# Attention's value products, low halves, key and query copies rebuilt in a two-layer decoder trunk on one core

## The chip, the cores and the metric

The kernel runs on one core of a Trainium2 chip. The metric is the device time of one execution in microseconds. A core has five engines with a queue of instructions each: TensorE (PE, matmuls; its loads of stationary operands are listed as PEld), VectorE (DVE), ScalarE (ACT), GpSimd (POOL) and SyncE (SP), which here only issues DMAs.

## The reference

512 tokens of width 1024 go through two layers. Layer 0 mixes tokens with a gated MLP in chunks of 128. After it, one shared set of keys and values is computed. Layer 1 attends to it. Both layers also have a gated convolutional MLP of width 2816 and a gated per-layer embedding; everything is float32. The part that the change touches:

```python
kv = rmsnorm(h, g) @ w_kv                       # 4 key/value heads of 64
q = (xn @ w_q).reshape(B, nb, BLOCK, 4, 4, 64)  # 16 query heads, 4 to a group
scores = einsum('bnikgd,bnjkd->bnkgij', q, kblk) * 64 ** -0.5
scores = scores - slopes * dist                 # window of 128, blocks of 128: previous and own
scores = where(valid, scores, -inf)
m = maximum(max(scores, -1), sink)
e = exp(scores - m)
probs = e / (sum(e, -1) + exp(sink - m))
out = einsum('bnkgij,bnjkd->bnikgd', probs, vblk)
return out.reshape(B, S, 1024) @ w_o
```

## The kernel before

Activations lie with features on the partitions and the 512 tokens along the free dimension, as eight row blocks of 128x512. Every float32 product is made of matmuls in the faster float32r form: each operand is split into a high half (the value rounded) and a low half (what is left), and `mm3` adds three products: high by high, high by low, low by high. So one 128x128 block of weights costs three matmuls of 512 columns.

Weights come as a stream of pieces of 1 MB. `load` issues a piece's DMA on SP into one of three raw buffers (two during attention, when the third holds the values). `pump` splits a piece in units of 128x1024: ACT casts the high half `wh` (L141), DVE subtracts for the low half `wl` (L142). There are four buffers for the units of each half, and a product asks for units four ahead.

Layer 1 starts with the key projection `k` (two tiles of 128 features), then the first group's queries `q`. `Norm.split` prepares the queries' input row blocks, `begin` and `rstd` give the norm's factor. Keys are kept per group in `kh` and `kl`: a group's 64 key features stand twice on the 128 partitions, so that a query tile whose upper half holds the high halves and whose lower half holds the low halves is multiplied with both at once. ACT makes both copies of the high halves (L536), DVE one and GpSimd the other copy of the low ones (L538). `queries` scales a query tile (L516) and writes the two halves with ACT (L521) and DVE (L522).

Attention proper has 16 steps, one for each of 4 groups of heads and 4 blocks of tokens, in a software pipeline written out by hand:

- `scores(i)`: two matmuls for each of four heads (L617, L618), then on DVE one instruction per head that adds the distance, scales, and takes the maximum (L620); `neg` (L624); four exponentials on ACT (L627) with their sums.
- `weights(i)`: sums and reciprocal on DVE (L637, L638), then the scaling of four heads, two on DVE (L644) and two on ACT (L642).
- `turn(i-1)`: transposes on PE (L654), then the split of the transposed probabilities into `ph` (ACT, L214) and `pl` (DVE, L215).
- `mix(i-2)`: for each key block three matmuls with 64 value columns (L671 to L673), into 64 partitions; then per head a cast on ACT (L678) and a subtraction on DVE (L679) into the input of the output projection `o2`.

Between these, `fill(i)` takes products that need no result of the step from the table `beside`: the value products (`values`, 256 columns per matmul), the next groups' query products (`project`) and, in the last steps, parts of the output projection (`merge`, tile `o`). After step 16 the rest of the output projection follows, 120 matmuls in a row.

Each engine works through its queue in order. The order in a queue is made ahead of time by the framework: by program order, with parts marked `high_priority` ahead, and by its own estimate of when an instruction can start. So the order on PE mixes fills, logits, transposes and value products.

Of the kernel before, what the change touches and what calls it, by code (L numbers as in the profile page):

```python
# [8 lines left out]
F32 = mybir.dt.float32  # L9
F32R = mybir.dt.float32r  # L10
# [36 lines left out]
def tile_yoco(ctx: ExitStack, tc: tile.TileContext, t, out: bass.AP, out_b: bass.AP):  # L47
# [14 lines left out]
    # ---- weights: a stream of pieces, each loaded once and split in two float32r halves  # L62
    pieces = []

    def plan(ap_, n, cols, own=None):
# [7 lines left out]
        pieces.append((ap_, n, cuts, own))  # L73

    def plan_cols(w, n_chunks, kk, cols=256, k0=0):
        for c in range(n_chunks):
            plan(w[c, :, k0 * cols : (k0 + kk) * cols], kk * cols, cols)
# [26 lines left out]
    plan_cols(t["w_q"][1:4], 3, KD)  # L104
    plan_cols(t["w_o"], 4, KD)
# [22 lines left out]
    def pump(upto):  # L128
        while state["unit"] < min(upto, len(units)):
# [12 lines left out]
            nc.vector.tensor_sub(wl[:, :n], src, wh[:, :n].bitcast(F32))  # L142
# [9 lines left out]
    def chunk(cols, kk, ahead=WBUFS):  # L152
        """The next units that make up kk row blocks of `cols` columns, a triple for each."""
# [8 lines left out]
    def mm3(ps, parts, xs, c0, n=P, first=True, last=True):  # L162
        """ps += W[:, c0:c0+n]^T x over the row blocks, as three float32r passes."""
# [8 lines left out]
    def mm3t(ps, xs, parts, c0, n, tok, first=True, last=True):  # L172
        """ps += x[tokens]^T W[:, c0:c0+n]: tokens on partitions."""
# [9 lines left out]
    # ---- activations in  # L183
# [24 lines left out]
    # ---- helpers on activations  # L208
# [16 lines left out]
    class Norm:  # L225
        """Takes the residual's row blocks as they come: gains and splits them, sums the squares."""
# [24 lines left out]
        def begin(self):  # L251
            """One over the root mean square, tokens on the partitions."""
# [6 lines left out]
        def rstd(self):  # L259
            """The same along the free dimension, for every partition."""  # L260
# [12 lines left out]
    def spread(r, n, name):  # L273
        """[P, n] with tokens on the partitions -> [P, n * P], the tokens along it, in PSUM."""
# [18 lines left out]
    def dense_add(xs, kk, norm):  # L293
        """h += W^T x for the next kk row blocks of weights, 256 columns a chunk."""
# [10 lines left out]
    def ffn(l, norm, nxt):  # L305
        """Gated MLP, the hidden units in parts; the first of the next part goes before a part's products down."""
# [79 lines left out]
    # ---- layer 0: gMLP mixer  # L386
# [26 lines left out]
    # minus the distance to the key, far away where the window or causality forbids it  # L413
# [7 lines left out]
    # queries over eight times a head's slope: logit = slope * (q k - distance)  # L421
# [10 lines left out]
    # positions attend to earlier ones alone: wsT[s, h, t] for s <= t  # L432
# [55 lines left out]
    # ---- layer 1: shared K/V and sliding-window attention  # L488
# [3 lines left out]
    # keys of a group, their halves twice on the partitions, for the stacked halves of the queries  # L492
# [14 lines left out]
    qps = psum("q0_0")  # L507
    mm3(qps, parts, xq, 0)
    rstd = nm.rstd()

    def queries(ps, g, j):
        """Two heads' queries, scaled for the distances; a head's tile has one half on its own
        partitions and the other half on the other's."""
# [3 lines left out]
        res = []  # L517
        for e in range(2):
            q = tp.tile([P, S], F32R, tag=("hs", "sg", "c0", "c1")[2 * j + e], name=f"q{g}_{j}_{e}")
            me, it = sides[e], sides[1 - e]  # L520
            nc.scalar.copy(q[me, :], qf[me, :])  # L521
            nc.vector.tensor_sub(q[it, :], qf[me, :], q[me, :].bitcast(F32))  # L522
            res.append(q)
# [3 lines left out]
    for j in range(2):  # L527
        if j:
            qps = psum("q0_1")
            mm3(qps, parts, xq, P)  # L530
        kf = tp.tile([P, S], F32, tag="acc", name=f"kf{j}")
        nc.vector.tensor_mul(kf, kps[j], rstd)
        for e in range(2):
            me = sides[e]
            for side in (me, sides[1 - e]):
                nc.scalar.copy(kh[j][side, e, :], kf[me, :])  # L536
            for side, eng in ((me, nc.vector), (sides[1 - e], nc.gpsimd)):
                eng.tensor_sub(kl[j][side, e, :], kf[me, :], kh[j][me, e, :].bitcast(F32))  # L538
        qs[0] += queries(qps, 0, j)
    state["tags"] = [0, 1]  # L540

    vt = wp.tile([P, 2, NC, 256], F32R, tag="r2", bufs=1, name="vt")

    # products beside attention's steps: each step is followed by some that need no result of it
    box = {}

    def values(c):
# [4 lines left out]
        nc.scalar.activation(vt[:, 0, c, :], ps[:, :256], AF.Copy, scale=rt[:, c : c + 1])  # L552
        nc.vector.scalar_tensor_tensor(vt[:, 1, c, :], ps[:, :256], rt[:, c : c + 1], vt[:, 0, c, :].bitcast(F32),
# [12 lines left out]
    def merge(m, k0, k1):  # L566
        """Row block m of the output projection, from the heads that are done."""
# [8 lines left out]
        -1: [(values, 0), (values, 1), (project, 1, 0, 0, 8)],  # L576
# [289 lines left out]
```

## Time and profile before

| | |
|---|---|
| median of 3 runs | 1174.45 us (1174.26 to 1174.66) |
| span of the profiled execution | 1173.3 us |
| PE, DVE, ACT, POOL busy | 1152.2, 761.8, 543.0, 80.7 us |
| mean granted TensorE clock | 0.996 |
| instructions | 14202 |

The profiled execution has no time of its own beside its span; the median of the runs is 1.15 us longer. Busy times of PE count overlapping instructions once; a matmul's recorded duration is longer than the distance to the next one. In a group's row, the mean is that of one instruction; the idle time is that of the engine just ahead of the group's instructions, with what ended it.

### The profile page before, as it was taken

Reading aid. Unit: us, or ns where it says so; the run is one execution under the profiler, and the core shown is the slowest. Engines: PE = TensorE matmul, PEld = TensorE weight load, DVE = VectorE, ACT = ScalarE, POOL = GpSimd, SP = SyncE. Lnnn points to the kernel's source line nnn. Section 1 sums busy time; section 2 is a strip of 40 time slices with the busy share of each in tenths; the row PEclk is TensorE's granted clock in tenths of the full one; section 3 lists DMA queues with packets and bytes.
Section 4 is the critical chain, followed back from the end, with each engine's and each line's share of the span. In section 5 each row is a group of like instructions: output and inputs, shape, how many; then the busy total and the mean of one; then the engine's idle time right before and its main releaser. Section 6 shows DMA issues by size and latency. Waiting matters only on the chain.

```text
span 1173.3 us, 14202 instructions
## 1 busy us (share of the span) xinstructions
PE 1152.2 (98%) x5634; PEld 968.3 (83%) x5634; DVE 761.8 (65%) x1229; ACT 543.0 (46%) x919; POOL 80.7 (7%) x86
## 2 busy tenths in 40 slices
PE   7999999999999999999989999999999999999998
PEld 7988888888888888888778767888888888888897
DVE  6365467763676377447779997577635773675665
ACT  5633444431344244445559986444313442345532
POOL 1000210000000000031220001100000000000221
PEclk9999999999999999999989999999999999999999
DMA  8222323322222333232212113322322333223302
GB/s 324 79 108 72 108 72 108 108 74 106 108 72 90 110 104 115 101 111 72 72 37 73 36 37 108 108 97 84 108 107 73 99 99 108 90 94 105 108 1 73
DMA packets 19011, 110.20 MB, mean 94 GB/s; under 512 B 2176, under 2 KB 3584, under 8 KB 8704
## 3 DMA queue, kind: packets, MB, share of 16 engines
q1 hardware_dynamic: 18112, 108.24, 26.5%
q10 hardware_dynamic: 832, 1.05, 0.3%
q8 instruction: 44, 0.72, 0.2%
q14 instruction: 23, 0.19, 0.1%
HBM read 107.19 MB, written 2.10 MB: 93 GB/s over the span
## 4 chain that ended last, share of the span: by engine, by line
PE 90%; DVE 6%; ACT 2%; issue 1%; DMA 0%; SPq 0%; POOLq 0%; POOL 0%; DVEq 0%; ACTq 0%
PE up L168 14%; PE up L170 14%; PE up L169 14%; PE d L168 8%; PE d L170 8%; PE d L169 8%; PE gate L169 2%; PE gate L168 2%; PE gate L170 2%; PE v L179 1%; PE v L180 1%; PE v L181 1%; PE u L168 1%; PE u L170 1%; PE u L169 1%; PE o L168 1%
## 5 line engine op out<-in xcount | busy, mean ns | idle before, releaser
L141 ACT CAST wh<-wraw 128x1024 fp32r<-128x1024 f32 (+1 forms) x198 | 203.0, 1026 | 272.8 <-PE d L169 132.2
L142 DVE TENSOR_TENSOR wl<-wraw,wh 128x1024 fp32r<-128x1024 f32 (+1 forms) x198 | 238.6, 1205 | 134.9 <-ACT wh L141 134.6
L168 PE MATMUL up<-nf00h,wh 128*128 128x512 f32 x352 | 137.2, 390 | 0.0
L168 PE MATMUL up<-nf10h,wh 128*128 128x512 f32 x352 | 137.2, 390 | 0.0
L170 PE MATMUL up<-nf10h,wl 128*128 128x512 f32 x352 | 137.1, 390 | 0.0
L170 PE MATMUL up<-nf00h,wl 128*128 128x512 f32 x352 | 137.1, 389 | 0.0
L169 PE MATMUL up<-nf00l,wh 128*128 128x512 f32 x352 | 137.1, 389 | 0.0
L169 PE MATMUL d<-al,wh 128*128 128x512 f32 x352 | 137.1, 389 | 0.0
L168 PE MATMUL d<-ah,wh 128*128 128x512 f32 x352 | 137.1, 389 | 0.0
L169 PE MATMUL up<-nf10l,wh 128*128 128x512 f32 x352 | 137.1, 389 | 0.0
L170 PE MATMUL d<-ah,wl 128*128 128x512 f32 x352 | 137.1, 389 | 0.0
L325 ACT ACTIVATE c<-hs,vec 128x512 f32<-128x512 f32 x88 | 71.5, 814 | 71.9 <-DVE hs L321 71.1
L326 DVE SCALAR_TENSOR_TENSOR c<-hs,vec,c 128x511 f32<-128x511 f32 x88 | 65.8, 749 | 34.2 <-ACT c L325 34.2
L301 DVE TENSOR_TENSOR h<-h,d 128x512 f32<-128x512 f32 x56 | 38.4, 687 | 73.7 <-PE d L170 73.7
L214 ACT CAST ah<-a 128x512 fp32r<-128x512 f32 x44 | 27.3, 621 | 109.1 <-DVE a L331 109.0
L170 PEld LDWEIGHTS up<-nf10h,wl 128*128 128x128 f32 x352 | 66.1, 188 | 13.8
L170 PEld LDWEIGHTS up<-nf00h,wl 128*128 128x128 f32 x352 | 66.1, 188 | 13.8
L170 PEld LDWEIGHTS d<-ah,wl 128*128 128x128 f32 x352 | 66.1, 188 | 13.7
L169 PEld LDWEIGHTS d<-al,wh 128*128 128x128 f32 x352 | 66.1, 188 | 13.7
L168 PEld LDWEIGHTS up<-nf00h,wh 128*128 128x128 f32 x352 | 66.1, 188 | 13.7
L169 PEld LDWEIGHTS up<-nf10l,wh 128*128 128x128 f32 x352 | 66.1, 188 | 13.6
L168 PEld LDWEIGHTS d<-ah,wh 128*128 128x128 f32 x352 | 66.1, 188 | 13.6
(281 smaller groups left out, 2195.4 us busy)
## 6 DMA issues: line engine op xcount, KB each, us to landing
wraw<-in_w_up SPq DMA_DIRECT2D x44, 1024.0 KB, 4.8
wraw<-in_w_down SPq DMA_DIRECT2D x16, 896.0 KB, 4.6
wraw<-in_w_down SPq DMA_DIRECT2D x8, 1024.0 KB, 4.9
wraw<-in_w_gate SPq DMA_DIRECT2D x8, 1024.0 KB, 4.8
wraw<-in_w_u SPq DMA_DIRECT2D x4, 1024.0 KB, 6.3
wraw<-in_w_out SPq DMA_DIRECT2D x4, 1024.0 KB, 4.7
wraw<-in_w_q SPq DMA_DIRECT2D x4, 1024.0 KB, 4.7
wraw<-in_w_o SPq DMA_DIRECT2D x4, 1024.0 KB, 4.8
```

The lines of the kernel that those rows point to most:

```text
L141: nc.scalar.copy(wh[:, :n], src)
L142: nc.vector.tensor_sub(wl[:, :n], src, wh[:, :n].bitcast(F32))
L168: nc.tensor.matmul(ps, wh[:, a:b], xh, start=st, stop=False)
L169: nc.tensor.matmul(ps, wh[:, a:b], xl, start=False, stop=False)
L170: nc.tensor.matmul(ps, wl[:, a:b], xh, start=False, stop=en)
L179: nc.tensor.matmul(ps, xh[:, s], wh[:, a:b], start=st, stop=False)
L180: nc.tensor.matmul(ps, xl[:, s], wh[:, a:b], start=False, stop=False)
L181: nc.tensor.matmul(ps, xh[:, s], wl[:, a:b], start=False, stop=en)
L214: nc.scalar.copy(hi, src)
L301: nc.vector.tensor_add(h[m], h[m], ps)
L325: nc.scalar.activation(c, hs, AF.Identity, bias=v("conv_b", l * 2 * NJ + col), scale=cw[2])
L326: nc.vector.scalar_tensor_tensor(c[:, 1:], hs[:, : S - 1], cw[1], c[:, 1:], op0=ALU.mult, op1=ALU.add)
```

## The change

- `mix`: the value tile holds a group's high and low halves side by side (`vt` is `[P, NC, GROUPS, 2, HD]`), so that one matmul with 128 stationary columns gives the products with both halves on 128 partitions. Two matmuls per key block in place of three (the low by low product is now included). Then ACT copies the lower 64 partitions (`lo`), DVE adds the two halves into `of` (two additions over two heads each), ACT casts two 128x128 blocks and GpSimd subtracts for their low halves.
- `pump`: for the last three pieces of `w_q` and the four of `w_o` the low halves are subtracted on GpSimd in place of DVE.
- Keys: ACT and DVE write one copy of the halves, and eight DMAs write the other. The two key tiles' products run over row blocks 0 to 5 first and then 6 and 7; both query products of group 0 come before the keys are taken out of PSUM.
- Queries of groups 1 to 3: one cast and one subtraction over the whole tile, then four DMAs to the two heads' tiles. Group 0 is as before.
- The logits are kept negated: the scale's sign is turned, the minimum with `nsink` gives the negated maximum at once, and the exponential has a scale of -1. The instruction `neg` goes.
- `weights`: all four scalings on DVE.
- `beside`: the first query product of group 1 moves from before step 0 to step 0, the second's two parts are joined at step 1.

```diff
-    plan_cols(t["w_q"][1:4], 3, KD)
-    plan_cols(t["w_o"], 4, KD)
+    plan_cols(t["w_q"][1:4], 3, KD, side=True)
+    plan_cols(t["w_o"], 4, KD, side=True)
...
-            nc.vector.tensor_sub(wl[:, :n], src, wh[:, :n].bitcast(F32))
+            (nc.gpsimd if pieces[i][4] else nc.vector).tensor_sub(wl[:, :n], src, wh[:, :n].bitcast(F32))
...
+    nsink = const.tile([P, HEADS], F32, name="nsink")
+    nc.gpsimd.tensor_scalar_mul(nsink, sink, -1.0)
...
-    kps = []
-    for j in range(2):
-        ps = psum(f"k{j}")
-        mm3(ps, parts, xkv, j * P)
-        kps.append(ps)
-        for k in range(4 * j, 4 * j + 4):
-            nm.split(k, 1)
+    kps = [psum(f"k{j}") for j in range(2)]
+    for k0, k1 in ((0, 6), (6, KD)):
+        for j in range(2):
+            mm3(kps[j], parts[k0:k1], xkv[k0:k1], j * P, first=k0 == 0, last=k1 == KD)
+    for k in range(KD):
+        nm.split(k, 1)
     rt = nm.begin()
     parts = chunk(256, KD)
-    qps = psum("q0_0")
-    mm3(qps, parts, xq, 0)
+    qps = [psum(f"q0_{j}") for j in range(2)]
+    mm3(qps[0], parts, xq, 0)
     rstd = nm.rstd()
+    mm3(qps[1], parts, xq, P)
+    for j in range(2):
+        kf = tp.tile([P, S], F32, tag="acc", name=f"kf{j}")
+        nc.vector.tensor_mul(kf, kps[j], rstd)
+        for e in range(2):
+            nc.scalar.copy(kh[j][sides[e], e, :], kf[sides[e], :])
+            nc.sync.dma_start(kh[j][sides[1 - e], e, :].bitcast(F32), kh[j][sides[e], e, :].bitcast(F32))
+        for e in range(2):
+            nc.vector.tensor_sub(kl[j][sides[e], e, :], kf[sides[e], :], kh[j][sides[e], e, :].bitcast(F32))
+            nc.sync.dma_start(kl[j][sides[1 - e], e, :].bitcast(F32), kl[j][sides[e], e, :].bitcast(F32))
...
+        hi = tp.tile([P, S], F32, tag="acc", name=f"qhi{g}_{j}")
+        nc.scalar.copy(hi.bitcast(F32R), qf)
+        nc.vector.tensor_sub(qf.bitcast(F32R), qf, hi)
+        for e, q in enumerate(res):
             me, it = sides[e], sides[1 - e]
-            nc.scalar.copy(q[me, :], qf[me, :])
-            nc.vector.tensor_sub(q[it, :], qf[me, :], q[me, :].bitcast(F32))
-            res.append(q)
+            nc.sync.dma_start(q[me, :].bitcast(F32), hi[me, :])
+            nc.sync.dma_start(q[it, :].bitcast(F32), qf[me, :])
...
-        kf = tp.tile([P, S], F32, tag="acc", name=f"kf{j}")
-        nc.vector.tensor_mul(kf, kps[j], rstd)
-        for e in range(2):
-            me = sides[e]
-            for side in (me, sides[1 - e]):
-                nc.scalar.copy(kh[j][side, e, :], kf[me, :])
-            for side, eng in ((me, nc.vector), (sides[1 - e], nc.gpsimd)):
-                eng.tensor_sub(kl[j][side, e, :], kf[me, :], kh[j][me, e, :].bitcast(F32))
...
-        -1: [(values, 0), (values, 1), (project, 1, 0, 0, 8)],
-        0: [(project, 1, 1, 0, 4)],
-        1: [(project, 1, 1, 4, 8)],
+        -1: [(values, 0), (values, 1)],
+        0: [(project, 1, 0, 0, 8)],
+        1: [(project, 1, 1, 0, 8)],
...
-            nc.vector.tensor_tensor_reduce(out=pr[:, e, :nk], in0=far[:, k0:], in1=o, scale=slope(hd),
-                                           scalar=sink[:, hd : hd + 1], op0=ALU.add, op1=ALU.max,
-                                           accum_out=mx[:, e : e + 1])
-        neg = at.tile([P, GQ], F32, tag="neg", bufs=2, name=f"neg{i}")
-        nc.vector.tensor_scalar_mul(neg, mx, -1.0)
+            nc.vector.tensor_tensor_reduce(out=pr[:, e, :nk], in0=far[:, k0:], in1=o, scale=-slope(hd),
+                                           scalar=nsink[:, hd : hd + 1], op0=ALU.add, op1=ALU.min,
+                                           accum_out=neg[:, e : e + 1])
...
-            if e in (1, 3):
-                nc.scalar.activation(a, a, AF.Copy, scale=r)
-            else:
-                nc.vector.tensor_scalar_mul(a, a, r)
+            nc.vector.tensor_scalar_mul(a, a, r)
...
-            nc.tensor.matmul(ps[:HD, :], vh, ph, start=b == 0, stop=False)
-            nc.tensor.matmul(ps[:HD, :], vh, pl, start=False, stop=False)
-            nc.tensor.matmul(ps[:HD, :], vl, ph, start=False, stop=end)
+            vv = vt[:, c, g].rearrange("p x d -> p (x d)")
+            nc.tensor.matmul(ps, vv, ph, start=b == 0, stop=False)
+            nc.tensor.matmul(ps, vv, pl, start=False, stop=b == len(pts) - 1)
         cols = slice(n * P, (n + 1) * P)
-        for e in range(GQ):
-            oh, ol = o2[2 * g + e // 2]
-            src = ps[:HD, e * P : (e + 1) * P]
-            nc.scalar.copy(oh[sides[e % 2], cols], src)
-            nc.vector.tensor_sub(ol[sides[e % 2], cols], src, oh[sides[e % 2], cols].bitcast(F32))
+        of = at.tile([P, 2, P], F32, tag="of", bufs=1, name=f"of{i}")
+        lo = at.tile([HD, S], F32, tag="olo", bufs=1, name=f"olo{i}")
+        nc.scalar.copy(lo, ps[sides[1], :])
+        halves = [a.rearrange("p (b e t) -> p b e t", b=2, e=2) for a in (ps[sides[0], :], lo)]
+        for e in range(2):
+            nc.vector.tensor_add(of[sides[e]], halves[0][:, :, e, :], halves[1][:, :, e, :])
+        for b in range(2):
+            oh, ol = o2[2 * g + b]
+            nc.scalar.copy(oh[:, cols], of[:, b, :])
+            nc.gpsimd.tensor_sub(ol[:, cols], of[:, b, :], oh[:, cols].bitcast(F32))
```

The rest of the diff takes comments and docstrings out.

More of the change, by code (lines that the diff above doesn't have):

```diff
@@ L63, in tile_yoco, with plan @@
     pieces = []
-    def plan(ap_, n, cols, own=None):
+    def plan(ap_, n, cols, own=None, side=False):
         if own and len(own) > 1:
@@ L516, in queries @@
         nc.vector.scalar_tensor_tensor(qf, ps, qscale[:, m : m + 1], rstd, op0=ALU.mult, op1=ALU.mult)
-        res = []
-        for e in range(2):
-            q = tp.tile([P, S], F32R, tag=("hs", "sg", "c0", "c1")[2 * j + e], name=f"q{g}_{j}_{e}")
+        res = [tp.tile([P, S], F32R, tag=("hs", "sg", "c0", "c1")[2 * j + e], name=f"q{g}_{j}_{e}")
+               for e in range(2)]
+        if g == 0:
+            for e, q in enumerate(res):
+                me, it = sides[e], sides[1 - e]
+                nc.scalar.copy(q[me, :], qf[me, :])
+                nc.vector.tensor_sub(q[it, :], qf[me, :], q[me, :].bitcast(F32))
+            return res
+        hi = tp.tile([P, S], F32, tag="acc", name=f"qhi{g}_{j}")
+        nc.scalar.copy(hi.bitcast(F32R), qf)
+        nc.vector.tensor_sub(qf.bitcast(F32R), qf, hi)
+        for e, q in enumerate(res):
             me, it = sides[e], sides[1 - e]
-            nc.scalar.copy(q[me, :], qf[me, :])
-            nc.vector.tensor_sub(q[it, :], qf[me, :], q[me, :].bitcast(F32))
-            res.append(q)
+            nc.sync.dma_start(q[me, :].bitcast(F32), hi[me, :])
+            nc.sync.dma_start(q[it, :].bitcast(F32), qf[me, :])
         return res
```

26 lines of the change are left out of this document (11 added, 15 removed).

## The prediction

> **What bounds the kernel now.** I read the page's engine shares and clock row first, then the windows by stage, then who TensorE (PE) waited for.
>
> ```profile
> span 1173.3 us, 14202 instructions
> PE 1152.2 (98%) x5634; PEld 968.3 (83%) x5634; DVE 761.8 (65%) x1229; ACT 543.0 (46%) x919; POOL 80.7 (7%) x86
> PEclk9999999999999999999989999999999999999999
> ```
>
> TensorE is busy everywhere; only one slice of 40 shows a lowered clock, near 600 us, where attention begins. The change touches the stretch from the key projection to the output projection, so I cut it into windows. Columns: window, length, then busy time (and instructions) of PE, PEld, DVE, ACT, POOL, the granted clock, DMA share and GB/s.
>
> ```profile
> 200.00:300.00 100.00, 100.00 (x443) 82.86 (x442) 56.81 (x68) 33.21 (x40) 0.00 (x0) 1.00 0.28 101
> ...
> 565.00:601.60 36.60, 32.28 (x169) 26.96 (x167) 31.18 (x44) 21.83 (x32) 10.45 (x7) 0.99 0.10 31
> 600.80:607.60 6.80, 5.97 (x16) 4.91 (x17) 2.91 (x16) 2.44 (x11) 0.00 (x0) 0.50 0.46 154
> 601.60:626.00 24.40, 24.37 (x135) 21.42 (x136) 15.94 (x56) 15.35 (x45) 0.00 (x0) 0.88 0.20 72
> 626.00:674.00 48.00, 46.93 (x258) 36.77 (x256) 45.77 (x159) 42.57 (x135) 0.00 (x0) 1.00 0.15 51
> 674.00:714.00 40.00, 38.25 (x194) 27.90 (x193) 34.50 (x125) 32.59 (x108) 0.00 (x0) 1.00 0.13 41
> 714.00:741.00 27.00, 27.00 (x120) 22.05 (x119) 19.34 (x26) 14.82 (x25) 8.59 (x6) 1.00 0.38 137
> ```
>
> The dense row at 200 gives the true price of a 512-column matmul: 100 us / 443 = 0.226 us (recorded durations near 0.39 us overlap). From 626 to 714 three engines run level: PE 85.2, DVE 80.3, ACT 75.2 of 88 us. So a step of attention has no single limit; PE ends last by a little. The row at 600.8 is the half clock: 6.8 us at 0.50 lose 3.4 us. From 714 on PE is saturated again, with 27 us of output projection that need little of anyone.
>
> ```profile
> PE sc L617 <- DVE mx L620: 2.5, 2, 2.1
> PE sc L617 <- DVE q L522: 2.0, 2, 1.6
> PE gate L169 <- DVE np10l L211: 1.3, 1, 1.3
> PE k L168 <- ACT n10h L210: 0.7, 1, 0.7
> PE sc L617 <- DVE pl L215: 0.4, 1, 0.4
> PE o L168 <- DVE mx L620: 0.4, 1, 0.4
> PE o L168 <- ACT oh L678: 0.3, 1, 0.3
> PE o L168 <- DVE ds L637: 0.2, 1, 0.2
> PE o L168 <- DVE pl L215: 0.2, 1, 0.2
> ```
>
> Columns: waiter and releaser, total, times, longest. Without the gate's row (another stage) PE idles 6.7 us here. The two longest, 1.6 and 2.1, are the first logits, just ahead of the half clock. Hence the start of attention costs 1.6 + 2.1 + 3.4 = 7.1 us, the key projection 0.7, and all later steps together 2.3 of recorded waits.
>
> **The change part by part.** Prices come from the groups of 545 to 725 us (count | busy us, mean ns):
>
> ```profile
> L142 DVE TENSOR_TENSOR wl<-wraw,wh 128x1024 fp32r<-128x1024 f32 x22 | 28.9, 1314 | 1.4 <-ACT wh L141 1.2
> L215 DVE TENSOR_TENSOR pl<-tr,ph 128x512 fp32r<-128x512 f32 x28 | 19.1, 687 | 2.3 <-ACT ph L214 2.1
> L679 DVE TENSOR_TENSOR ol<-pv,oh 64x128 fp32r<-64x128 f32 x64 | 17.3, 280 | 2.8 <-ACT oh L678 1.6
> L671 PE MATMUL pv<-ph,vt 128*64 128x512 f32 x28 | 11.1, 397 | 0.0
> L522 DVE TENSOR_TENSOR q<-qf,q 64x512 fp32r<-64x512 f32 x16 | 12.0, 748 | 0.4
> L642 ACT ACTIVATE pr<-pr,ds 128x256 f32<-128x256 f32 x24 | 10.8, 502 | 1.7 <-DVE ds L638 1.6
> L644 DVE TENSOR_SCALAR pr<-pr,ds 128x256 f32<-128x256 f32 x24 | 7.3, 348 | 0.0
> L538 DVE TENSOR_TENSOR kl<-kf,kh 64x512 fp32r<-64x512 f32 x4 | 5.5, 1374 | 0.1
> L624 DVE TENSOR_SCALAR neg<-mx 128x4 f32<-128x4 f32 x16 | 2.5, 158 | 0.1
> L644 DVE TENSOR_SCALAR pr<-pr,ds 128x128 f32<-128x128 f32 x8 | 1.9, 280 | 0.1
> ```
>
> *Value products in two passes.* The third matmul of each of 28 key blocks goes. The two that stay are as long (512 columns), with 128 weight columns in place of 64. 28 x 0.226 = 6.3 us leave PE. This shortens the span only as far as PE sets the pace: bounds -6.3 and 0; I take -6.3 and charge the other engines' slowness below.
>
> *Combining the halves.* DVE loses 64 subtractions (-17.3) and gains 32 additions of 64x256 with one operand in PSUM. The nearest rows are 280 ns at 128 columns and 687 at 512, so 0.42 us each, +13.3. ACT trades 64 short casts for 16 of 64x512 and 32 of 128x128, about even. The 32 low halves go to GpSimd.
>
> *Weights all on DVE.* 24 x 0.348 + 8 x 0.280 = +10.6 us; ACT loses the same scalings (24 x 0.50 = 12 and eight short ones).
>
> *Negated logits.* 16 x 0.158 = -2.5 us on DVE, taken out of the chain from maximum to exponential; the sink's negation is one small GpSimd instruction in layer 0, long before anyone reads it: nil.
>
> *Weights' low halves on GpSimd.* Seven pieces of two units: 14 x 1.22 (undisturbed, fence below) = -17.1 us on DVE.
>
> *Queries of groups 1 to 3.* 12 half-height subtractions become 6 full ones at 0.69: -4.1 us on DVE.
>
> DVE's sum is 13.3 + 10.6 - 17.3 - 2.5 - 17.1 - 4.1 = -17.1 us, if GpSimd does not disturb it. What GpSimd takes on:
>
> ```profile
> L739 POOL TENSOR_TENSOR facc<-fsq,fsq 128x256 f32<-128x256 f32 x2 | 1.5, 736 | 12.3 <-ACT fsq L732 10.2 <-PE gate L170 2.1
> L244 POOL TENSOR_TENSOR nf1acc<-nf1sq,nf1sq 128x512 f32<-128x512 f32 x1 | 1.3, 1332 | 126.8 <-DVE nf10l L211 126.8
> ```
>
> 736 ns at 256 columns and 1332 at 512 put 1024 columns near 2.6 us and 128 near 0.44: 14 x 2.6 + 32 x 0.44 = 50 us of GpSimd, most of it between 601.6 and 714, where the windows show none now. And a GpSimd instruction is not free for DVE. From two stretches of the timeline (start, duration):
>
> ```profile
> 543.95 1.22 DVE L142 TENSOR_TENSOR wl<-wraw,wh 128x1024 fp32r<-128x1024 f32 x1
> ```
> ```profile
> 546.91 1.33 POOL L244 TENSOR_TENSOR n1acc<-n1acc,n1sq 128x512 f32<-128x512 f32 x1 [4.15 <-ACT n1sq L239]
> ```
> ```profile
> 547.02 2.32 DVE L142 TENSOR_TENSOR wl<-wraw,wh 128x1024 fp32r<-128x1024 f32 x1
> ```
> ```profile
> 566.95 1.53 POOL L244 TENSOR_TENSOR n1acc<-n1acc,n1sq 128x512 f32<-128x512 f32 x1 [3.84 <-ACT n1sq L239]
> ```
> ```profile
> 567.25 0.68 DVE L378 TENSOR_TENSOR z<-gate,np0rstd 128x512 f32<-128x512 f32 x1
> ```
>
> The subtraction that started under the GpSimd addition took 2.32 instead of 1.22 us: it ended 1.1 us after that addition did, as if it had only then begun. The product at 567.25, one operand in PSUM, was not touched. So what reads two SBUF operands waits out GpSimd. In the new step those are the small sums for the denominator and the query subtraction; the new additions and the logits read PSUM. The Trainium skill ("SBUF — State Buffer", section "SBUF: two separate sides") says that the pair of ports is an exclusive lock held for the whole instruction, against DVE instructions with two SBUF inputs and also against those in a two-port mode; the first half agrees with 2.32 beside 1.22, and for the second, which would take in the weights' scalings, no row here has an overlap.
>
> Price: 16 steps lie in those 112 us, 7 us each, with about 2.4 groups of such instructions (denominator's two sums, and six query subtractions over all). A 2.6 us GpSimd instruction is met with a chance near 0.6, for 1.4 us on average: 14 x 0.6 x 1.4 = 12, and 1 for the short ones. Bounds 0 and 50; I take 13, nearest to half of each 2.6. DVE then gets 17.1 - 13 = 4 us shorter while PE gets 6.3 shorter: DVE becomes the engine that ends a step. I hand back the difference of 2.3, and 1.2 for half as many uneven waits again as today's 2.3: +3.5 (bounds -1.5, if those waits shrink instead, and +14).
>
> *Start of attention.* The six first row blocks of both key tiles now run before the last two, which hides PE's 0.7: -0.7. Keys are doubled by eight DMAs instead of ACT and GpSimd copies. The four DVE subtractions at 1374 ns sat under GpSimd's share and return to 0.69, -2.7 us, but two of the weights' low halves now fall there. One group of DMA rows bounds the new latency:
>
> ```profile
> out<-y SPq DMA_DIRECT2D x4, 256.0 KB, 2.5
> ```
>
> That is to DRAM; 128 KB inside SBUF should land in 1.5 to 2.5 us. I take 2. All eight lie beside the remaining query product and the 48 short value products. Moving the next query product (24 x 0.226 = 5.4 us) behind the first logits removes no work; it takes cover from the wait and gives it to the first step. I leave 1.7 of the 3.7 us of idling: -2.0 (bounds -3.7 and +2). With 1.7 us the clock should hold, since the gate's single wait of 1.3 lowered nothing that the clock row shows: -3.4 (bounds -3.4 and 0). The Trainium skill ("TensorE: Matmul & The Clock Gate", section "What's actually happening") puts the drop behind an idle window of about 3.4 us; here 1.6 and 2.1 us with work between them were enough, so by the trace a stall of half that is the safer reading.
>
> *New waits.* The second unit of the third query piece can only be split after the last value product has freed its buffers, and its low half takes 2.6 instead of 1.2 us: +1.0 (0 to +3). Behind a group's last value product stand ACT copy, two additions, cast and a GpSimd subtraction before the output projection may use it, on a PE that is in order: +1.5 (0 to +4). Query DMAs sit in the SP queue among the weight loads, with two steps (14 us) until they are needed: 0. After 714 the 27 us of saturated PE hide the longer last chain: 0.
>
> Sum: -6.3 + 3.5 - 0.7 - 2.0 - 3.4 + 1.0 + 1.5 = -6.4. 1173.3 - 6.4 = 1166.9 of span; the median shown is 1.15 above the profiled span, so 1168.0.
>
> **The rivals.** *GpSimd's lock sets the pace.* If each of the 14 instructions holds DVE for its full 2.6 us, DVE gets 36 - 17 = 19 us longer; between 626 and 714 it has 8 us free, the start still gives about 5: +6, 1180. It decides from about 30 us of holding, 2.1 us per instruction. For it: the lock above, and scalings of all four heads exposed. Against: most of DVE's work reads PSUM. *Queries come late.* SP's queue waits long in front of weight loads:
>
> ```profile
> SPq L124 <- DVE wl L142: 246.8, 18, 30.5
> ```
>
> If a query's copy stands behind such a load, up to 30 us against 14 of slack, PE would stall for 5 to 15 us at two group changes: 1180 to 1195. Against: the queue has nothing else now, so long waits cost nothing and say little on order. *PE keeps the pace.* No hand-back, half the new waits, no idling at the start: -6.3 - 0.7 - 7.1 + 1 = -13.1, 1161. For it: ACT loses 12 us and more of scalings, DVE 17. *Eaten.* DVE or the chain keeps the step as long as before, and the clock still drops: -0.7 - 2 + 1 = -1.7, 1172.7; the change does not reach the span.
>
> **How the numbers follow.** Forecast 0.46, PE keeps the pace 0.17, eaten 0.14 (a third of it beyond the bound), lock 0.13, late queries 0.10. A measurement can tell 0.2%, 2.3 us. Faster 0.68, same 0.10, slower 0.22. The range goes from 1159, below the best case by its bounds, to 1181, past the lock; the forecast's own is 1163 to 1172.
>
> **What would show it.** Right: 28 fewer matmuls; no half clock near 600; DVE groups with SBUF operands lengthened, GpSimd near 55 us; the wait at the first logits under 2 us. Wrong: a clock of 0.50 again after 590; PE waiting for a query's DMA; DVE over 95% busy with denominators of 1 to 2 us; windows from 626 on as long as now.

## The result and the profile after

The changed kernel took 1177.95 us (median of 6 runs, 1177.25 to 1181.8); the kernel before took 1174.68 us beside it. The ratio is 1.0032, 95% interval 1.0022 to 1.0042: slower by 3.3 us, where 6.4 us faster was forecast.

Two profiles were taken of the changed kernel. The first is of the longest execution, 1181.8 us (span 1180.1), which ran 17.1 us at half clock in three stretches, 8.5 us lost. The second, 1176.41 us with a span of 1174.7, lies nearer to the median and is read below as "after". Its busy times:

```profile
PE 1146.4 (98%) x5606; PEld 966.8 (82%) x5606; DVE 760.5 (65%) x1193; ACT 528.6 (45%) x861; POOL 126.2 (11%) x129
```

TensorE has 28 matmuls fewer and 5.8 us less to do, as planned. DVE has 36 instructions fewer, yet its busy time has hardly moved (761.8 before, 760.5 now). GpSimd went from 80.7 to 126.2 us. The prediction's windows, with the same columns, and a last one for the whole stretch from 626:

```profile
565.00:601.60 36.60, 33.10 (x168) 28.55 (x167) 29.36 (x51) 20.79 (x36) 9.73 (x5) 0.95 0.30 87
601.60:626.00 24.40, 22.14 (x139) 19.54 (x138) 18.64 (x52) 13.40 (x36) 4.97 (x3) 1.00 0.24 52
626.00:674.00 48.00, 42.77 (x235) 34.29 (x234) 44.72 (x137) 34.43 (x102) 17.51 (x17) 1.00 0.32 95
674.00:714.00 40.00, 36.06 (x184) 28.33 (x183) 31.63 (x110) 28.55 (x88) 14.14 (x19) 0.96 0.13 40
626.00:714.00 88.00, 78.83 (x416) 62.62 (x415) 76.36 (x246) 62.98 (x189) 31.65 (x36) 0.98 0.23 70
```

From 626 to 674 PE is busy 42.8 us where it had 46.9: it idles. DVE, at 44.7 of 48, has not come down, although ACT now has 8 us less and GpSimd 17.5 us where it had none. The clock is below 1 twice, 0.95 and 0.96: two stretches of 3.4 us at half speed, one from 598 us and one from 683.6. Together they cost what the one stretch of 6.8 us cost before. Who PE waited for (545 to 750 us; total, times, longest):

```profile
PE sc L632 <- DVE neg L635: 10.1, 8, 2.5
PE o L169 <- ACT oh L692: 2.1, 1, 2.1
PE sc L632 <- DVE q L536: 1.0, 1, 1.0
PE sc L632 <- DMA q<-qf: 0.8, 1, 0.8
PE sc L632 <- DVE pl L216: 0.3, 1, 0.3
PE o L170 <- POOL ol L693: 0.3, 1, 0.3
```

These waits make 14.6 us; before they made 6.7. That closes the account: 6.3 us of matmuls gone, 7.9 us of waits added, the loss to the clock the same: +1.6, where the span grew by 1.4. It is the account of this execution; the median run is 1.5 us longer, and the two runs on either side of it have granted clocks of 0.995 and 0.993 beside 0.996 here, so part of that is clock. Most of the new waits are at the logits. These need a bank of PSUM that DVE frees when it has reduced the logits before (`neg`, line 635), and DVE is late. The groups say why:

```profile
L143 POOL TENSOR_TENSOR wl<-wraw,wh 128x1024 fp32r<-128x1024 f32 x14 | 35.0, 2503 | 50.9 <-ACT wh L142 50.9
L654 DVE TENSOR_SCALAR pr<-pr,ds 128x256 f32<-128x256 f32 x48 | 21.3, 501 | 0.2
L693 POOL TENSOR_TENSOR ol<-of,oh 128x128 fp32r<-128x128 f32 x32 | 14.7, 479 | 48.6 <-ACT oh L692 48.6
L689 DVE TENSOR_TENSOR of<-pv,olo 64x256 f32<-64x256 f32 x32 | 13.2, 413 | 3.2 <-POOL ol L693 2.6 <-ACT olo L686 0.2
L650 DVE TENSOR_TENSOR ds<-ds,sm 128x4 f32<-128x4 f32 x16 | 7.3, 462 | 4.2 <-ACT ds L644 3.9
L536 DVE TENSOR_TENSOR q<-qf,q 64x512 fp32r<-64x512 f32 x4 | 5.5, 1364 | 0.8 <-ACT q L535 0.7
```

A sum of four numbers for each partition (line 650) takes 462 ns. The weights' scaling (line 654) takes 501 ns; it took 348. The query subtraction takes 1364; untouched it takes 686 (in a_wl_dve below). The sum took 157 ns before:

```profile
L637 DVE TENSOR_TENSOR ds<-ds,sm 128x4 f32<-128x4 f32 x16 | 2.4, 157 | 3.8 <-ACT ds L631 3.8
```

Over their counts that is 48 x 0.153 + 16 x 0.305 + 4 x 0.678 = 14.9 us, and 0.5 more for the short scalings: DVE is held for 15.4 us. The addition with one operand in PSUM (line 689) takes 413 ns, as priced. One hold can be followed through three engines of this profile (start, duration). GpSimd:

```profile
590.75 5.45 POOL L143 TENSOR_TENSOR wl<-wraw,wh 128x1024 fp32r<-128x1024 f32 x2 [11.14 <-ACT wh L142]
```
```profile
625.96 2.41 POOL L143 TENSOR_TENSOR wl<-wraw,wh 128x1024 fp32r<-128x1024 f32 x1 [6.85 <-ACT wh L142]
628.33 0.98 POOL L693 TENSOR_TENSOR ol<-of,oh 128x128 fp32r<-128x128 f32 x2
629.27 2.42 POOL L143 TENSOR_TENSOR wl<-wraw,wh 128x1024 fp32r<-128x1024 f32 x1
```

DVE, beside these:

```profile
592.64 4.11 DVE L536 TENSOR_TENSOR q<-qf,q 64x512 fp32r<-64x512 f32 x2 [0.69 <-ACT q L535]
```
```profile
626.51 1.88 DVE L650 TENSOR_TENSOR ds<-ds,sm 128x4 f32<-128x4 f32 x1 [0.36 <-ACT ds L644]
628.42 0.18 DVE L651 RECIPROCAL ds<-ds 128x4 f32<-128x4 f32 x1
628.64 3.47 DVE L654 TENSOR_SCALAR pr<-pr,ds 128x256 f32<-128x256 f32 x4
```

PE, behind these:

```profile
594.04 0.33 PE L632 MATMUL sc<-kh,q 128*128 128x128 f32 x1 [1.03 <-DVE q L536]
```
```profile
597.58 0.33 PE L632 MATMUL sc<-kh,q 128*128 128x128 f32 x1 [2.47 <-DVE neg L635]
```
```profile
633.41 0.33 PE L632 MATMUL sc<-kh,q 128*128 128x128 f32 x1 [2.32 <-DVE neg L635]
```
```profile
682.84 0.50 PE L169 MATMUL o<-oh,wh 128*128 128x512 f32 x1 [2.06 <-ACT oh L692]
```

A GpSimd subtraction ran from 625.96 to 628.37. DVE's four-column sum began at 626.51 and ended at 628.39, as that subtraction did. Then came the reciprocal and the four scalings, which are held in turn by the second subtraction, from 629.27 to 631.69 (3.47 us, where four free ones at 606.34 took 1.14). Behind them in DVE's queue, after two other instructions, stood the reduction of the next logits, and PE stood for 2.32 us. At 592.64 it is the same with the two query subtractions: 4.11 us in place of 1.41 for the two before them, PE waits 1.03 and 2.47, and then the clock falls. The last row is another matter: the output projection waits for the chain behind a group's last value product, and the second stretch at half clock follows it.

### The profile page after: what moved, and what is told of

It reads as the page before. It is cut to its first block, busy times and chain, and to the rows that moved or that the text cites. A ratio compares the mean times of both kernels' runs of the same rounds, so it can differ in the third digit from the quotient of the medians.

```text
span 1180.1 us, 14226 instructions
## 1 busy us (share of the span) xinstructions
PE 1151.1 (98%) x5606; PEld 970.3 (82%) x5606; DVE 760.6 (64%) x1193; ACT 528.7 (45%) x861; POOL 126.3 (11%) x129
## 4 chain that ended last, share of the span: by engine, by line
PE 91%; DVE 5%; ACT 2%; issue 1%; DMA 1%; SPq 0%; POOLq 0%; POOL 0%; DVEq 0%; ACTq 0%
PE up L169 14%; PE up L171 14%; PE up L170 14%; PE d L170 8%; PE d L171 8%; PE d L169 8%; PE gate L170 2%; PE gate L169 2%; PE gate L171 2%; PE v L180 1%; PE v L181 1%; PE v L182 1%; PE u L170 1%; PE u L171 1%; PE u L169 1%; DVE pr L654 1%
## 5 line engine op out<-in xcount | busy, mean ns | idle before, releaser
L143 DVE TENSOR_TENSOR wl<-wraw,wh 128x1024 fp32r<-128x1024 f32 (+2 forms) x184 | 221.8, 1206 | 134.4 <-ACT wh L142 134.2
L170 PEld LDWEIGHTS up<-nf00l,wh 128*128 128x128 f32 x352 | 66.1, 188 | 13.6
```

The source lines that it names most:

```text
L143: (nc.gpsimd if pieces[i][4] else nc.vector).tensor_sub(wl[:, :n], src, wh[:, :n].bitcast(F32))
L170: nc.tensor.matmul(ps, wh[:, a:b], xl, start=False, stop=False)
```

## The experiments

**The theories.** The first is the lock: a GpSimd instruction stops DVE's work on SBUF operands until it ends, and DVE's fixed order passes the stop on to PE. The rivals: that scalings which ACT shared are now all on DVE; that the two-pass products trade a dense stretch of PE for a longer chain of additions; that queries or keys come late by DMA. The kernels come in two lines, from the one after and from the one before, and later from the fastest found. The kernel before was run again beside each group of kernels, with medians from 1174.43 to 1174.97 us, so a comparison across groups carries some 0.5 us.

**Low halves back on DVE (a_wl_dve).** One word of the change undone:

```
- (nc.gpsimd if pieces[i][4] else nc.vector).tensor_sub(wl[:, :n], src, ...)
+ nc.vector.tensor_sub(wl[:, :n], src, ...)
```

> The changed kernel with the weights' low halves back on DVE (14 subtractions of 128x1024), all else changed. Theory L (the lock): GpSimd's 14 long instructions hold DVE in lumps of up to 2.5 us (scalings L654 501 ns on average beside 344 undisturbed, sums L650 461 beside 163, query subtractions L536 1360 beside 686: some 15 us in all), and PE, which waits in order for the logits' PSUM, loses the lumps: without them DVE gets 17 us of work and loses 15 us of holding, but evenly; PE's waits at sc fall from 10 us to 3 or 4, time 1169 to 1172. Theory C (the chain): the new step itself (four scalings on DVE, the longer way through the halves' addition) makes DVE late; then DVE only gets more work and the time stays at 1177 to 1180. Theory Q (queries by DMA): no change, 1177 to 1179.

Measured: 1169.14 us, ratio 0.9950 (0.9937 to 0.9962), 8.8 us below the changed kernel and within the lock's forecast. Its busy times and groups:

```profile
PE 1145.0 (98%) x5606; PEld 965.8 (83%) x5606; DVE 760.7 (65%) x1207; ACT 530.1 (45%) x861; POOL 92.7 (8%) x115
```
```profile
L654 DVE TENSOR_SCALAR pr<-pr,ds 128x256 f32<-128x256 f32 x48 | 15.1, 374 | 0.2
L650 DVE TENSOR_TENSOR ds<-ds,sm 128x4 f32<-128x4 f32 x16 | 2.9, 192 | 2.3 <-ACT ds L644 2.0
L536 DVE TENSOR_TENSOR q<-qf,q 64x512 fp32r<-64x512 f32 x4 | 2.7, 686 | 0.1
```

DVE does 14 subtractions more than in the changed kernel and is busy for the same time, 760.7 beside 760.5. So the move to GpSimd had relieved DVE of nothing, and had put its time in worse places. The waits at the logits fell from 10.1 to 2.2 us:

```profile
PE o L169 <- ACT oh L692: 3.2, 1, 3.2
PE sc L632 <- DVE neg L635: 2.2, 5, 0.7
```

**Only the low halves, on the kernel before (b_wl_pool).** The opposite: the kernel before with `side=True` on the same seven pieces and nothing else.

> The kernel before with only the weights' low halves of the last three query pieces and of the output projection on GpSimd. Theory L: DVE loses 17 us of work, but two scalings, the small sums and 12 query subtractions per stage are held; slower than before by 1 to 6 us, with lengthened L644, L637 and L522. Theory C: DVE is relieved and nothing else is changed, so 1 to 4 us faster than before. Theory Q: as C.

Measured: 1190.02 us, ratio 1.0129 (1.0115 to 1.0143), 15.2 us slower. Its groups:

```profile
L522 DVE TENSOR_TENSOR q<-qf,q 64x512 fp32r<-64x512 f32 x16 | 18.9, 1180 | 0.4
L644 DVE TENSOR_SCALAR pr<-pr,ds 128x256 f32<-128x256 f32 x24 | 13.7, 614 | 0.1
L624 DVE TENSOR_SCALAR neg<-mx 128x4 f32<-128x4 f32 x16 | 6.8, 424 | 0.2
```

Queries 748 to 1180 ns, scalings 348 to 614, the negation of four columns 158 to 424: these three groups are held 17.6 us. So the lock shows in the rows, but its forecast of 1 to 6 us was far too small. The edit alone also costs more than inside the change (15.2 beside 8.8 us). It meets six query subtractions and 16 negations more, though 32 scalings fewer; which of these makes the difference isn't shown.

**Useless work on GpSimd (a_dummy).** a_wl_dve, whose DVE work stays as it is, plus 14 GpSimd subtractions whose results nobody reads:

```
  nc.vector.tensor_sub(wl[:, :n], src, wh[:, :n].bitcast(F32))
+ if pieces[i][4]:
+     nc.gpsimd.tensor_sub(src, src, wh[:, :n].bitcast(F32))
```

> The changed kernel with the weights' low halves back on DVE (1169.1), and GpSimd doing 14 subtractions of the same shape whose result nobody reads: it takes the unit's high half from its raw buffer in place, after DVE has made the real low half. DVE's and PE's own work is that of the kernel at 1169.1; GpSimd's is that of the changed kernel. If the hold on DVE is the cause, scalings and small sums are lengthened again, up to 2.5 us, and the time rises by 8 us or more (DVE has 17 us more work than in the changed kernel): 1177 to 1186. If the loss came from the low halves being ready later, or from another order of the queues: 1168 to 1171.

Measured: 1181.43 us, ratio 1.0050 (1.0036 to 1.0064), 12.3 us more than without them. Its busy times, groups and PE's waits:

```profile
PE 1149.3 (97%) x5606; PEld 969.1 (82%) x5606; DVE 775.3 (66%) x1207; ACT 528.6 (45%) x861; POOL 130.0 (11%) x129
```
```profile
L145 POOL TENSOR_TENSOR wraw<-wraw,wh 128x1024 f32<-128x1024 f32 x14 | 35.2, 2511 | 39.5 <-DVE ds L652 13.7 <-DMA kl<-kl 13.5 <-DVE wl L143 10.2
L656 DVE TENSOR_SCALAR pr<-pr,ds 128x256 f32<-128x256 f32 x48 | 19.1, 454 | 0.2
```
```profile
PE sc L634 <- DVE neg L637: 8.9, 8, 2.4
PE o L171 <- ACT oh L694: 5.1, 1, 5.1
```

DVE executes the same 1207 instructions and is busy for 14.6 us more. Nothing computes with what GpSimd leaves; only the loads of later weights wait for the buffer, and no wait of PE in this stretch is for a weight. PE's long waits, in the last two rows, are for DVE and for ACT behind DVE. The one of 5.1 us can be followed: a GpSimd subtraction ran from 678.48 to 680.82, and DVE's four-column sum under it until 680.84.

```profile
678.65 2.19 DVE L652 TENSOR_TENSOR ds<-ds,sm 128x4 f32<-128x4 f32 x1 [0.45 <-ACT ds L646]
```

Only then came the two additions, ACT's cast at 681.92, and PE at 682.27. One rival is left to weigh: GpSimd's own low halves of the outputs (`ol`) stand behind the long instructions, and DVE's additions wait for them, as there is one buffer. But DVE waits 2.3 us for `ol` there with the idle work and 2.3 without it. So it is not that a result comes late from a slower engine: GpSimd's being busy costs the time.

**The same work in shorter instructions (a_wl_half).** The changed kernel, each low half as two subtractions of 512 columns.

```
+ for x in (slice(0, n // 2), slice(n // 2, n)):
+     nc.gpsimd.tensor_sub(wl[:, x], src[:, x], wh[:, x].bitcast(F32))
```

> The changed kernel with each of GpSimd's 14 low halves cut into two instructions of 512 columns (some 1.25 us each in place of 2.5): the same GpSimd work, lumps half as long. If the length of a lump is what costs (an engine in order behind one wait of 2.5 us, PE behind it, then the half clock), PE's waits at sc fall from 10 us by half and the time goes to 1172 to 1175. If the sum of GpSimd's occupation is what costs, 28 shorter holds add up to the same 15 us on DVE and the time stays at 1176.5 to 1179.

Measured: 1173.68 us, ratio 0.9992 (0.9983 to 1.0001), 4.3 us below the changed kernel and within the first of the two forecasts, for 2.5 us more GpSimd work:

```profile
L145 POOL TENSOR_TENSOR wl<-wraw,wh 128x512 fp32r<-128x512 f32 x28 | 37.5, 1358 | 49.3 <-ACT wh L142 49.3
L658 DVE TENSOR_SCALAR pr<-pr,ds 128x256 f32<-128x256 f32 x48 | 20.8, 490 | 0.2
L654 DVE TENSOR_TENSOR ds<-ds,sm 128x4 f32<-128x4 f32 x16 | 5.4, 339 | 4.1 <-ACT ds L648 3.8
L540 DVE TENSOR_TENSOR q<-qf,q 64x512 fp32r<-64x512 f32 x4 | 4.5, 1126 | 0.8 <-ACT q L539 0.7
```

The three groups are held 11.5 us in all, where they were held 14.9. The waits for `neg` went from 10.1 to 6.4 us, the longest from 2.5 to 1.9. Both the sum of the holds and the longest hold fell, so the run doesn't tell which of the two counts; it shows that the same GpSimd work costs less in shorter instructions.

**Two of four scalings back on ACT, with GpSimd's low halves (a_wts_split) and without (a_wl_dve_wts).**

```
- nc.vector.tensor_scalar_mul(a, a, r)
+ if e in (1, 3): nc.scalar.activation(a, a, AF.Copy, scale=r)
+ else: nc.vector.tensor_scalar_mul(a, a, r)
```

> The changed kernel with two of the four scalings back on ACT. Theory L: half of the scalings' exposure to the lock goes, 3 to 4 of the 7.5 us of holding, the sums stay held: 1174 to 1176.5. Theory C: DVE gets 10.6 us shorter and its burst ahead of the transposes half as long, so most of the loss goes: 1169 to 1173. Theory Q: 1176 to 1178.

> The changed kernel with the low halves back on DVE and two of the four scalings back on ACT: DVE 10.6 us shorter than with the low halves alone (1169.1), ACT 13.6 longer. If DVE's work now sets the step: 1164 to 1167. If the order of the queues sets it (a product of the output projection that waits 3.2 us for its cast, queries that come by DMA): 1168 to 1170. If ACT becomes the bound, as in the value products taken alone (1176.6): 1171 to 1175.

Measured: 1175.52 us, ratio 1.0007 (0.9998 to 1.0016), with the lock still there, 2.4 us gained, within the lock's forecast; 1162.84 us, ratio 0.9904 (0.9891 to 0.9918), without it, 6.3 us gained, 1.2 us past the best that was forecast. So both edits of the change on DVE's and GpSimd's shares cost time, the lock first. The second kernel is the fastest found, 15.1 us below the changed one; below I call it the best. Its busy times, the window from 626 and the longest waits:

```profile
PE 1144.1 (98%) x5606; PEld 965.4 (83%) x5606; DVE 752.2 (65%) x1175; ACT 539.6 (46%) x893; POOL 93.2 (8%) x115
```
```profile
626.00:714.00 88.00, 85.31 (x438) 68.21 (x437) 74.52 (x227) 74.11 (x215) 18.31 (x32) 0.98 0.26 82
```
```profile
PE sc L632 <- DVE neg L635: 1.2, 3, 0.6
```

PE is busy for 85.3 of the 88 us, with 438 matmuls where the changed kernel had 416, and all its waits between 545 and 750 us make 3.0 us. (This profile is of the longest of its four executions, 1164.42 us; its 0.98 is one stretch of 3.4 us.)

**The two-pass products, alone and from the other end (b_mix, best_mix3).** The first is the kernel before with the new layout of the values, two passes and the new combining (with the outputs' low halves on GpSimd); the second is the best with the three passes and combining of before.

> The kernel before with only the value products in two passes, their combination on ACT and DVE and the low halves of the outputs on GpSimd; all else as before. 28 matmuls fewer, 6.3 us. Theory L: only short GpSimd instructions are added (0.48 us), so most of it shows: 1168 to 1171. Theory C: the longer chain to the output projection and the shared single buffers eat it: 1173 to 1177. Theory Q: 1168 to 1171.

> The fastest version so far (low halves of the weights on DVE, two scalings on ACT, 1162.8) with the value products in three passes and their splitting by head on ACT and DVE as in the kernel before. 28 matmuls more, 6.3 us; DVE +4 us; the chain to the output projection shorter. If PE sets the pace in that version: 1168 to 1171. If the combination of the halves costs what the matmuls spare, as it did when taken alone (1176.6 beside 1174.8): 1161 to 1164.

Measured: b_mix 1176.61 us, ratio 1.0014 (1.0005 to 1.0023), 1.8 us slower; best_mix3 1173.20 us, ratio 0.9986 (0.9978 to 0.9995), 10.4 us slower than the best. The first lies where the longer chain had been forecast, not the lock; the second is 2.2 us above its forecast. The same edit costs 1.8 us in one kernel (the interval of its ratio starts at 1.0005, close to no change) and saves 10.4 us in the other. The window from 674 of b_mix, and the busy times of best_mix3:

```profile
674.00:714.00 40.00, 33.84 (x167) 26.71 (x166) 32.53 (x107) 33.78 (x104) 7.21 (x16) 0.91 0.08 27
```
```profile
PE 1151.0 (98%) x5634; PEld 968.2 (83%) x5634; DVE 752.3 (64%) x1207; ACT 539.1 (46%) x909; POOL 74.8 (6%) x83
```

In both the clock was 0.91 in this window (3.6 of 40 us lost). In b_mix it fell behind one long stall, where DVE was late with the scaled weights that PE transposes:

```profile
PE tr L656 <- DVE pr L646: 7.1, 5, 4.7
```

Undoing the edit in the best adds 6.9 us to PE's busy time (1144.1 to 1151.0), of which the 28 matmuls are 6.3, and 2.4 us of idling; that makes the 9.3 us between the two spans, 1162.5 and 1171.8. Its waits from 545 to 750 us went from 3.0 to 6.8 us. So most of what the edit saves there is PE's own work, the rest stalls and clock. In b_mix PE's waits went from the 6.7 us of the kernel before to 12.9. That DVE and ACT, both level with PE in that window, make the longer chain cost more there is the likely reason, and isn't shown by itself.

**The other steps, undone one by one.** Three kernels: a_wl_dve with the queries of groups 1 to 3 made by ACT and DVE again (`if g == 0:` to `if True:`, a_wl_dve_qeng); a_wl_dve with the outputs' low halves on DVE (`nc.gpsimd` to `nc.vector` at line 693, a_wl_dve_ol); and the best with the start of attention as it was before: key tiles one after the other, keys doubled by copies, the second query product behind the first keys, the next group's query product ahead of the first logits (best_start).

> The changed kernel with the low halves back on DVE and the queries of groups 1 to 3 made by ACT and DVE as for group 0, with no DMA. DVE +4.1 us, ACT +3.7 us against the low halves alone (1169.1); PE's waits for a query's DMA (0.8 us) go. If the DMAs spare the engines as meant: 1170 to 1173. If their latency and their place behind weight loads cost as much as they spare: 1168 to 1169.5.

> The changed kernel with the low halves of the weights and also those of attention's outputs back on DVE: GpSimd has nothing left between 601 and the end of attention. DVE +32 x 0.29 = 9 us against the low halves of the weights alone (1169.1), holds of up to 0.5 us (some 1.5 us in all) go. If DVE's work sets the step: 1172 to 1175. If short holds too cost PE a lump each: 1167 to 1169.

> The fastest version so far (1162.8) with the start of attention as in the kernel before: key tiles one after the other, both copies of the keys by ACT, DVE and GpSimd, the second query product behind the first keys, the next query product ahead of the first logits. By the prediction's own steps the start is worth 0.7 + 2.0 + 3.4 = 6.1 us: 1168 to 1170, with waits of 1.6 and 2.1 us and a half clock of 6.8 us near 600. If the earlier start is given back in later steps: 1163 to 1165.

Measured: a_wl_dve_qeng 1172.93 us, ratio 0.9988 (0.9979 to 0.9997), 3.8 us above a_wl_dve; a_wl_dve_ol 1173.10 us, ratio 0.9989 (0.9981 to 0.9998), 4.0 us above it; best_start 1168.32 us, ratio 0.9944 (0.9932 to 0.9956), 5.5 us above the best. So each kernel is slower with its step undone, once the long low halves are off GpSimd, and the three times lie where the first of the forecasts put them. In best_start the old waits of 1.6 and 2.1 us and the stretch of half clock are back (0.87 from 601.6 to 626). In a_wl_dve_ol the forecast was met by luck: it was to be DVE's work, but DVE is busy for only 4.3 us more, while PE waited 6.3 us for queries' DMAs (0.8 in a_wl_dve) and the clock was 0.87 from 674 to 714. So its 4.0 us is the price of the order that came out, more than of 32 subtractions.

**The changed kernel once more (after_again).** No edit.

> The changed kernel once more, for a second profile: the profiled execution of the first (1181.8) lies 3.9 us above the median of six, with three stretches of half clock. If those stretches come and go with PE's waits, this one has one or two of them, 1177 to 1179, and the same waits of 1 to 2.5 us at sc on DVE; if they belong to the kernel, three again and 1181 to 1182.

Measured: 1176.41 us, the profile shown above, a little under the forecast for fewer stretches. Two executions of one kernel differ by 5.4 us: 2 x 3.4 us of half clock here, 17.1 us in the first, which is 5.2 us more lost ((17.1 - 6.8) / 2). PE's waits for `neg` are the same in both, 10.0 and 10.1 us in eight waits of up to 2.5. The wait of 2.3 us near 633 is in both too; behind it the clock stayed at 1.00 in the second profile and fell for 6.8 us in the first:

```profile
634.06 0.47 PE L632 MATMUL sc<-kh,q 128*128 128x128 f32 x1 [2.30 <-DVE neg L635]
```
```profile
633.80:637.20 3.40, 3.14 (x9) 2.67 (x10) 3.13 (x15) 2.84 (x12) 0.23 (x1) 0.50 0.74 289
```

So the stalls belong to the kernel, but whether the clock falls behind one of them differs from execution to execution, and that makes the kernel noisy: its six runs spread over 4.6 us, the five of a_wl_dve over 0.4.

## Why the prediction was wrong, point by point

**The step that failed is the hand-back of +3.5 us, the lock's share in DVE's sum.** Its inputs were right: GpSimd takes 2.50 and 0.48 us (2.6 and 0.44 forecast), 49.7 us in all (50), and holds DVE for 15.4 us (13). But I spread the 13 us over DVE's total, set 17.1 us of saved subtractions against it, and got 4 us of relief (DVE's busy time fell by 1.3). In the trace the saved time and the held time are not exchangeable. With the 14 subtractions on DVE, PE waits 2.2 us for `neg`; with them on GpSimd it waits 10.1, since the holds fall on the sum, the scalings and the query subtraction, behind which logits and PE wait in order. Taking the long low halves off GpSimd gave 8.8 us with 17 us more work for DVE; adding them as idle work cost 12.3 us for 14.6 us of DVE time. So five sixths of the hold came through to the span in that run, where I let 3.5 of 13 through. That the 13 came near 15.4 is partly luck: it was reckoned without the scalings, and it is 0.9 us per instruction, not the half of 2.6 that I called it.

**Which instructions are held** was half right. I priced the sums and the query subtractions and left the scalings out; they are half of the hold (7.8 of 15.4 us). The Trainium skill ("SBUF — State Buffer", section "SBUF: two separate sides") had them in: its lock is also against DVE instructions in a two-port mode. With 501 beside 348 ns for the scalings, and 424 beside 158 for a negation of four columns, these runs agree with that half. The trace before had no overlap to show it, but it had a hint: from 128 to 256 columns a scaling grew from 280 to 348 ns, 0.53 ns a column, and a subtraction from 512 to 1024 columns from 687 to 1220 ns, 1.04 a column. To read the faster rate as the two-port mode is my inference.

**The start of attention** (-0.7, -2.0, -3.4) was right as a mechanism: undone in the best it costs 5.5 of the 6.1 us. It failed in the changed kernel: there the two GpSimd instructions at 590.75 sat on the query subtractions, PE waited 1.0 and 2.5 us (1.6 and 2.1 before), and the clock fell. I had named the two instructions and given them no price there.

**The account.** The terms for waits came to +3.3 (hand-back 3.5, start -2.7, new waits 2.5); they measured +7.9. The term for the clock was -3.4; it measured 0. Those two misses, 4.6 and 3.4, make the distance between the forecast span of 1166.9 and the 1174.7 of the second profile. The lock is behind the first and behind the stretch of half clock at 598: a_wl_dve, without it, waits 2.2 us for `neg`, and its clock is 1.00 there (window below). The second stretch, at 683.6, follows the output projection's wait of 2.1 us. I had priced that wait (+1.5), not the clock that may fall behind it.

```profile
565.00:601.60 36.60, 35.62 (x189) 30.23 (x188) 31.39 (x64) 23.43 (x42) 4.26 (x3) 1.00 0.29 87
```

**The other terms.** Two passes: -6.3 of matmuls is there, and additions at 413 ns (420). Their bound, that this shortens the span only as far as PE sets the pace, proved decisive: 1.8 us lost on the kernel before, 10.4 gained in the best. Weights all on DVE: 10.6 us more for DVE were taken as paid by the other savings, the same error as with the lock; they cost 6.3 us of span even with the weights' low halves back on DVE, while ACT had room (busy 63.0 of 88 us from 626 to 714). New waits: the third query piece shows no row (+1.0 forecast). DMAs: 128 KB land in 2.3 us (2 taken), and PE waited 0.8 us for one (0).

**The rivals.** What came is "GpSimd's lock sets the pace" (0.13), in a milder form than its 1180. Its threshold was wrong: it was to decide from 30 us of holding, 2.1 us per instruction, because I measured the hold against DVE's free time over 88 us. It decided at 15.4 us, 1.1 per instruction. "Eaten" (0.14) fits the clock that still fell, but not its reason: the step had room, as the best shows. Queries did not come late in this order, though in a_wl_dve_ol they did (6.3 us). "PE keeps the pace" (1161) is what the best does (1162.84), with the two edits undone that I had thought helped it.

**The signs I had named.** 28 fewer matmuls and lengthened SBUF groups came true; a clock that holds near 600 and a wait under 2 us at the first logits did not (2.5 us). Of the signs against, a clock of 0.50 after 590 came, and windows from 626 on as long as before: the last value product ended at 715.7 us, 714.1 before. PE waited for a query's DMA once, 0.8 us. Denominators of up to 1.88 us came, DVE over 95% busy did not: it stood at 87% from 626 to 714. So DVE held PE up here at that share, since its work comes in bursts.

**What stays open.** Differences between these kernels of about 1 us can come from the order in which the planner puts instructions, which every edit shifts, so the prices above don't add up exactly. The 1 us is a guess, not measured. Why the clock fell behind some stalls and not behind others, and whether the length of one hold or the sum of all counts more, stays open. Whether 256-column low halves on GpSimd would beat DVE wasn't tried.

## What to carry to other kernels

Before moving elementwise work from DVE to GpSimd, list which DVE instructions in that stage read and write SBUF only, and who stands behind them in order: here each GpSimd instruction could hold the next of those until it ended, so price each against the burst that it may hit, not the sum against DVE's average. If GpSimd must be used there, use short instructions: half the length gave back 4.3 of the 8.8 us. To put the long ones into a stage where DVE reads PSUM or nobody waits is the other way, which no run here tried. And a step that frees an engine is worth something only while that engine sets the pace: the same two-pass products lost 1.8 us and gained 10.4.

## What the hardware showed that I had not expected

DVE gained nothing at all from 14 subtractions fewer: 760.5 us busy with them on GpSimd, 760.7 with them on DVE. A sum of four columns took up to 1.88 us, an instruction of 0.16 us otherwise, and a scaling with a single tensor operand is held as well.

The clock fell behind less idling than one long gap: after waits of 1.0 and 2.5 us with seven matmuls in a stretch of 3.4 us (593.4 to 596.8, PE busy for 1.08), and after 0.32, 2.06 and 0.28 us close together (680 to 684). But the amount of idling alone doesn't decide it: the wait of 2.3 us near 633 lowered nothing in the second profile (PE busy for 1.08 of the 3.4 us from 630.5) and was followed by 6.8 us at half clock in the first. The stretches at half clock were 3.4 or 6.8 us long. The Trainium skill ("TensorE: Matmul & The Clock Gate", section "What's actually happening") puts the fall behind an idle window of about 3.4 us; the lengths agree with that window, and the runs add that the window need not be empty.
